# Holding each block of 128 queries in reverse, so that the relative-bias table loads from its 12 rows

## The chip, the cores and the metric

The kernel runs on one core of a Trainium2 chip. Times are device microseconds of one execution; lower is better. A core has TensorE (matmuls, PE in the profile; its weight loads are PEld), VectorE (DVE), ScalarE (ACT), GpSimd (POOL), and SyncE (SP), which here issues nearly all DMA transfers from one queue, in order.

## The reference

Two layers of an encoder over 256 tokens of 1024 channels, in float32. Each layer runs three token mixers side by side (differential attention with 4 heads, a gated DeltaNet, windowed attention with 8 heads), merges them, and then runs a gated MLP. The change concerns the bias that the two attentions add to their scores. It depends only on key position minus query position:

```python
rel = key_pos[None, :] - (start + jnp.arange(Q_BLOCK))[:, None]
bias = bias_table[t5_bucket(rel)].astype(jnp.float32).transpose(2, 0, 1)
p = jax.nn.softmax(s + bias[None, :, None], axis=-1)
```

There are 12 heads, so 12 rows of 511 different values. The windowed attention also masks distances over 128.

## The kernel before

**Work and precision.** All activations stay on the chip; the weights come from memory in blocks of 128 x 1024 floats (512 KB, the tile `raw`, three buffers). ScalarE rounds a block to `hi`, VectorE subtracts to get the residual `lo` (four buffers each), and TensorE multiplies each product in three passes (`mm3`). A block of a projection takes 24 matmuls of 256 columns. `weights` and `take` do this; their rows are `hi_take<-raw_take`, `lo_take<-raw_take,hi_take` and `mm_proj_ch`.

**Order.** Nothing is issued as it is written. `Plan` records every operation with a cost, dependencies and a rank, and `schedule` then lays out one order for all five engines; each engine runs its list in that order. `ORDER` gives the list of projections of each layer (the two lists are the same up to the eleventh entry and differ in a few places behind it), `PRIO` shifts ranks by label. A transfer from SP is priced by its output's elements, x 4 / 3.6e5 us, with 0.91 us until it lands; the blocks of weights are ahead of other transfers by `BOOST`. All lines of the profile are line 191, where the recorded call is made; so one goes by tiles.

**The bias table.** `bias_table` multiplies a one-hot matrix (33 x 512) by the table, copied eight times (`tbx`, 96 columns), so that the 12 rows lie on 96 partitions. Twelve transfers, one a head, then write each row 128 times into `skew` in device memory, with a pitch of 513 floats (256 KB a head). `load_G` reads it with a pitch of 512: each partition's row starts one element earlier than the one before, which is the shift from query to query. The result is a tile `G` of 128 queries x 384 keys (192 KB, two buffers), 24 times: 12 heads in each of two layers. Both blocks of queries read from the same tile, 128 columns apart.

**Where the queries go.** `stacked` copies the projected queries from PSUM into two tiles, q + residual stacked in the halves of the partitions. It serves the differential attention (tile `q_stacked`) and the window (`h_stacked`). In `attention` and `window` the scores of a block land with its queries on the partitions, VectorE adds G and takes the maximum, and after softmax and the product with the values the result is transposed back and written as a rounded half and a residual (`yh`, `yl`; tiles `ya_attention`, `yc_window`).

Of the kernel before, what the change touches and what calls it, by code (L numbers as in the profile page):

```python
# [10 lines left out]
F32 = mybir.dt.float32  # L11
# [4 lines left out]
ALU = mybir.AluOpType  # L16
# [3 lines left out]
P = 128  # L20
# [461 lines left out]
def tile_encoder_trunk(ctx: ExitStack, tc: tile.TileContext, a: dict, out: bass.AP, depth=DEPTH, tap=None):  # L482
    nc = tc.nc
    plan = Plan()
    A = plan.either(nc.scalar, nc.vector)
    tap_ = tap
    tap = lambda name, ap: tap_(name, ap, SY.dma_start) if tap_ else None
    V, S, G, TE, SY = [plan.engine(*e) for e in (("DVE", nc.vector), ("ACT", nc.scalar), ("POOL", nc.gpsimd), ("PE", nc.tensor), ("SP", nc.sync))]

    cp = ctx.enter_context(tc.tile_pool(name="cp", bufs=1))  # L490
# [4 lines left out]
    dp = ctx.enter_context(tc.tile_pool(name="dp", bufs=1, space=bass.MemoryType.DRAM))  # L495
# [4 lines left out]
    def nm(base):  # L500
        import sys
        f = sys._getframe(2)
        base = f"{base}_{f.f_code.co_name}{f.f_lineno}"
        counts[base] = counts.get(base, 0) + 1
        return f"{base}_{counts[base]}"
# [4 lines left out]
    def buf(tag, shape=(P, 512), dtype=F32):  # L510
        return plan.tile(mp, shape, dtype, tag, nm(tag), BUFS[tag])

    def small(cols, dtype=F32, tag=None):
        n = {"g16": 8, "bn": 2, "mv": 2, "ve": 2, "rs": 2, "nmr": 2, "g8": 1}.get(tag, 4)
        return plan.tile(sp, (P, cols), dtype, tag, nm("s"), n)
# [10 lines left out]
    def ps_at(shape=(P, 512), dtype=F32):  # L526
        return plan.tile(pm, shape, dtype, "at", nm("at"), BANKS["at"], True)
# [4 lines left out]
    def bc_mid(ap, n):  # L532
        return ap.unsqueeze(1).to_broadcast([ap.shape[0], n, ap.shape[1]])

    def bc_last(ap, n):
        return ap.unsqueeze(2).to_broadcast([ap.shape[0], ap.shape[1], n])

    def drow(ap, off, n):
        return bass.AP(ap.tensor, ap.offset + off, [[0, P], [1, n]])


    late = []

    def load(n, out, in_):

        late.append((SY.dma_start(out=out, in_=in_), LOADS[n - 9]))
# [18 lines left out]
    V.memset(nhalf, -0.5)  # L565


    skew = dp.tile([12, P * 513], F32, name="skew")

    def bias_table():  # L570
        oh = buf("yc", (33, 512))
        load(11, oh, a["onehot"])
        tb = cp.tile([33, 12], F32, name="tb")
        V.memset(tb[32:33, :], NEG)
        V.memset(tb[32:33, 0:4], 0.0)
        load(11, tb[0:32, :], a["rel_bias"])
        tbx = cp.tile([33, 8, 12], F32, name="tbx")
        V.tensor_copy(tbx, bc_mid(tb, 8))
        fps = ps_at()
        TE.matmul(fps[0:96, :], tbx.rearrange("p c h -> p (c h)"), oh, start=True, stop=True)  # L580
        fsb = buf("yc", (96, 512))
        A.copy(fsb, fps[0:96, :])
        for h in range(12):
            SY.dma_start(
                out=bass.AP(skew.tensor, skew.offset + h * P * 513, [[16 * 513, 8], [513, 16], [1, 512]]),
                in_=fsb[h:96:12, :].unsqueeze(1).to_broadcast([8, 16, 512]),
            )

    def load_G(h):
        t = buf("G", (P, 384))  # L590
        SY.dma_start(out=t, in_=bass.AP(skew.tensor, skew.offset + h * P * 513 + 127, [[512, P], [1, 384]]))
        return t


# [134 lines left out]
    def pow_nhalf(dst, src, n):  # L729
        G.tensor_tensor(dst, src, nhalf[:, 0:n], op=ALU.pow)  # L730
# [475 lines left out]
    HALVES = [slice(0, 64), slice(64, 128)]  # L1206

    def stacked(ps, tags):

        out = []  # L1210
        for g, tag in enumerate(tags):
            t = buf(tag, (P, 2, T), F32R)
            A.copy(t[HALVES[g]], ps[HALVES[g]])
            V.tensor_tensor(t[HALVES[1 - g]], ps[HALVES[g]], t[HALVES[g]].bitcast(F32), op=ALU.subtract)
            out.append(t)
        return out


    def attention(l, pr, ys):
        dq, dk, dl = [], [], []  # L1220
        for b in range(2):
            ps = yield "aq", b
            dq.append(stacked(ps, ("q", "q")))
            ps = yield "ak", b
            kh, kl = [[buf(PAIRS[b], (P, 2, T), F32R) for _ in range(2)] for _ in range(2)]
            for c, (t, u) in enumerate(zip(kh, kl)):
                for r in HALVES:
                    A.copy(t[r], ps[HALVES[c]])
                for r in HALVES:
                    V.tensor_tensor(u[r], ps[HALVES[c]], t[HALVES[c]].bitcast(F32), op=ALU.subtract)  # L1230
            dk.append(kh)
            dl.append(kl)
        dv = yield "av", 0
        yh = [buf("ya", (P, 2, T), F32R) for _ in range(2)]
        yl = [buf("ya", (P, 2, T), F32R) for _ in range(2)]
        for h in range(NH):
            plan.label = (l, "a", h)
            gt = load_G(h)
            es = []
            mx = small(4, tag="mx")  # L1240
            sm = small(4, tag="sm")
            for c in range(2):
                ps = ps_at((P, 2, T))
                e = buf("e", (P, 2, T))
                for s in range(2):
                    qb = 1 - s
                    q = dq[h // 2][c][:, h % 2, qb * P:(qb + 1) * P]
                    TE.matmul(ps[:, s], q, dk[h // 2][c][:, h % 2], start=True, stop=False)
                    TE.matmul(ps[:, s], q, dl[h // 2][c][:, h % 2], start=False, stop=True)
                for s in range(2):  # L1250
                    n = 2 * c + s
                    V.tensor_tensor_reduce(e[:, s], ps[:, s], gt[:, s * P:s * P + T], 1.0, NEG, ALU.add, ALU.max, mx[:, n:n + 1])
                V.tensor_scalar(mx[:, 2 * c:2 * c + 2], mx[:, 2 * c:2 * c + 2], -0.125, None, ALU.mult)
                for s in range(2):
                    n = 2 * c + s
                    S.activation(e[:, s], e[:, s], AF.Exp, scale=0.125, bias=mx[:, n:n + 1], accum_out=sm[:, n:n + 1])
                es.append(e)
            rs = small(4, tag="rs4")
            V.reciprocal(rs, sm)
            V.tensor_scalar(rs[:, 2:4], rs[:, 2:4], pr["nlam"], None, ALU.mult)  # L1260
            for s in range(2):
                A.scale(es[0][:, s], es[0][:, s], rs[:, s:s + 1])
                V.scalar_tensor_tensor(es[0][:, s], es[1][:, s], rs[:, 2 + s:3 + s], es[0][:, s], ALU.mult, ALU.add)
            pt = ps_at((P, 2, T))
            for s in range(2):
                for kb in range(2):
                    TE.transpose(pt[:, kb, (1 - s) * P:(2 - s) * P], es[0][:, s, kb * P:(kb + 1) * P], ident)
            aT = buf("aT", (P, 2, T))
            A.copy(aT, pt)
            po = ps_at((P, 2, P))  # L1270
            for qb in range(2):
                for kb in range(2):
                    TE.matmul(po[:, qb], aT[:, kb, qb * P:(qb + 1) * P], dv[kb][:, h * P:(h + 1) * P], start=kb == 0, stop=kb == 1)
            ss = small(2, tag="ss2")
            o = buf("o", (P, 2, P))
            for qb in range(2):
                S.activation(o[:, qb], po[:, qb], AF.Square, accum_out=ss[:, qb:qb + 1])
            V.tensor_scalar(ss, ss, 1.0 / P, RMS_EPS, ALU.mult, ALU.add)
            f = small(2, tag="f2")
            pow_nhalf(f, ss, 2)  # L1280
            V.tensor_tensor(o, po, bc_last(f, P), op=ALU.mult)
            py = ps_at((P, T))
            for qb in range(2):
                TE.transpose(py[:, qb * P:(qb + 1) * P], o[:, qb], ident)
            hs, ls = yh[h // 2][:, h % 2], yl[h // 2][:, h % 2]
            A.scale(hs, py, pr["subln"])
            V.scalar_tensor_tensor(ls, py, pr["subln"], hs.bitcast(F32), ALU.mult, ALU.subtract)
        tap(f"ya{l}", yh[0])
        tap(f"zza{l}", yl[0])
        ys[0] = yh, yl  # L1290


    def window(l, pr, ys):
        rows = HALVES
        sq = []
        for b in range(2):
            ps = yield "cq", b
# [4 lines left out]
        ps = yield "ckv", 0  # L1302
# [12 lines left out]
        yh = [buf("yc", (P, 2, T), F32R) for _ in range(2)]  # L1315
        yl = [buf("yc", (P, 2, T), F32R) for _ in range(2)]
        for t in range(4):
            plan.label = (l, "c", t)
            aTs = []
            for g in range(2):  # L1320
                h = g * 4 + t
                gt = load_G(NH + h)
                ps = ps_at((P, 2, T))
# [24 lines left out]
            po = ps_at((P, T))  # L1348
            for kb in range(2):
                for g in range(2):  # L1350
                    TE.matmul(po[g * 64:(g + 1) * 64], vt[:, kb, g * 64:(g + 1) * 64], aTs[g][:, kb], start=kb == 0, stop=kb == 1)
            hs, ls = yh[t // 2][:, t % 2], yl[t // 2][:, t % 2]
            A.copy(hs, po)
            V.tensor_tensor(ls, po, hs.bitcast(F32), op=ALU.subtract)
        tap(f"yc{l}", yh[0])
# [130 lines left out]
```

## Time and profile before

| | |
|---|---|
| three runs | 1022.42, 1021.48, 1022.13 us; median 1022.13 |
| profiled execution | 1024.28 us, its span 1022.6 us |
| mean granted TensorE clock in it | 0.994 |
| busy: TensorE, weight loads | 979.9 us, 912.4 us |
| busy: VectorE, ScalarE, GpSimd | 745.6, 577.7, 112.1 us |
| DMA | 168.55 MB, mean 165 GB/s, 4.19 MB of it written |

The span is what the profile covers of the execution; the rest lies around it. The profiled execution is one of its own, 2.15 us above the median. [...] Names in a row read out<-in, with the buffer numbers left out; x is the number of instructions.

### The profile page before, as it was taken

To read this page: it belongs to the slowest core of one execution; us is meant where nothing else is said; L and a number is where in the kernel's file an instruction comes from. 1 tells how busy PE (TensorE), PEld (TensorE's weight loads), DVE (VectorE), ACT (ScalarE), POOL (GpSimd) and SP (SyncE) were. 2 spreads that over 40 slices of the span, in tenths; PEclk is the share of its full clock that TensorE was granted. 3 is DMA by queue.
4 is the path that set the end of the run, shared out by engine and by line. 5 is a ranking of instruction groups with operands and counts; after the bars stand their busy time and mean duration, and the time that the engine had idled before them with its cause. 6 is when DMAs were issued, how large, how long until landed. Compare 5 with 4: busy or idle time off the path is not lost. (4 is left out here: it accounts for less than half of the span.)

```text
span 1022.6 us, 19176 instructions
## 1 busy us (share of the span) xinstructions
PE 979.9 (96%) x7598; PEld 912.4 (89%) x7598; DVE 745.6 (73%) x1327; ACT 577.7 (56%) x1024; POOL 112.1 (11%) x108
## 2 busy tenths in 40 slices
PE   7989999999998999999989999999999979999996
PEld 5889999998986999998869989999999869999885
DVE  6779977675489776665679998875657878666555
ACT  5647685676455565554435776766644626555432
POOL 0510002100005100000144200001000240000000
PEclk9999999999999999999999999999999999999998
DMA  7854433463563765565625444333546736566662
GB/s 227 254 184 128 141 108 130 138 201 123 170 226 121 217 204 185 184 186 185 207 82 165 145 132 140 94 114 123 181 136 195 232 138 193 181 186 184 188 198 67
DMA packets 51717, 168.55 MB, mean 165 GB/s; under 512 B 5835, under 2 KB 11355, under 8 KB 51628
## 3 DMA queue, kind: packets, MB, share of 16 engines
q1 hardware_dynamic: 50252, 162.91, 50.5%
q0 software_dynamic: 1376, 4.43, 1.5%
q8 instruction: 59, 0.97, 0.4%
q14 instruction: 30, 0.25, 0.1%
HBM read 163.12 MB, written 4.19 MB: 164 GB/s over the span
## 5 line engine op out<-in xcount | busy, mean ns | idle before, releaser
L191 PE MATMUL mm_proj_ch<-xTl,hi_take 128*128 128x256 f32 x1488 | 420.4, 286 | 4.5 <-DVE xTl L191 4.5
L191 PE MATMUL mm_proj_ch<-xTh,lo_take 128*128 128x256 f32 x1488 | 421.9, 286 | 1.1 <-DVE lo_take L191 1.1
L191 PE MATMUL mm_proj_ch<-xTh,hi_take 128*128 128x256 f32 x1488 | 421.8, 287 | 0.4 <-ACT hi_take L191 0.4
L191 DVE TENSOR_TENSOR lo_take<-raw_take,hi_take 128x1024 fp32r<-128x1024 f32 x219 | 271.9, 1247 | 124.4 <-ACT hi_take L191 113.9
L191 ACT ACTIVATE hi_take<-raw_take 128x1024 fp32r<-128x1024 f32 x213 | 225.6, 1059 | 240.7 <-PE mm_proj_ch L191 150.7
L191 PEld LDWEIGHTS mm_proj_ch<-xTl,hi_take 128*128 128x128 f32 x1488 | 283.8, 192 | 8.9 <-DVE xTl L191 5.8
L191 PEld LDWEIGHTS mm_proj_ch<-xTh,lo_take 128*128 128x128 f32 x1488 | 284.4, 192 | 3.9 <-DVE lo_take L191 2.5
L191 PEld LDWEIGHTS mm_proj_ch<-xTh,hi_take 128*128 128x128 f32 x1488 | 283.8, 192 | 2.1 <-ACT hi_take L191 0.8
L191 DVE TENSOR_TENSOR lo_proj_tok<-raw_proj_tok,hi_proj_tok 128x1024 fp32r<-128x1024 f32 x50 | 61.2, 1225 | 48.8 <-ACT hi_proj_tok L191 48.8
L191 ACT ACTIVATE hi_proj_tok<-raw_proj_tok 128x1024 fp32r<-128x1024 f32 x50 | 53.1, 1061 | 74.0 <-PE mm_run L191 33.8
L191 POOL TENSOR_TENSOR s_tail<-s_tail,nhalf 128x1 f32<-128x1 f32 x8 | 6.8, 854 | 370.8 <-DVE s_tail L191 370.8
L191 DVE SCALAR_TENSOR_TENSOR z_conv_silu<-mm_proj_ch,col_params,z_conv_silu 128x254 f32<-128x254 f32 (+1 forms) x96 | 39.8, 475 | 1.1 <-ACT z_conv_silu L191 1.0
L191 ACT ACTIVATE e_window<-e_window,s_window 128x256 f32<-128x256 f32 x57 | 27.2, 498 | 7.3 <-DVE s_window L191 7.2
L191 POOL DMA_DIRECT2D ya_ln_params<-in_lnp_dram x16 | 8.8, 552 | 188.8 <-PE mm_product L191 96.5
L191 DVE SCALAR_TENSOR_TENSOR g_product<-g_product,mm_product 128x512 f32<-128x512 f32 x24 | 16.3, 684 | 16.4 <-PE mm_product L191 16.2
L191 PE MATMUL mm_run<-hi_proj_tok,ile_encoder_trunk 128*128 128x512 f32 x88 | 27.3, 389 | 0.0
L191 PE MATMUL mm_run<-hi_proj_tok,tile_encoder_trunk 128*128 128x512 f32 x88 | 27.2, 389 | 0.0
L191 ACT ACTIVATE e_attention<-e_attention,s_attention 128x256 f32<-128x256 f32 x47 | 22.6, 500 | 4.8 <-DVE s_attention L191 4.8
L191 PE MATMUL mm_product<-yc_window,hi_take 128*128 128x256 f32 x128 | 24.1, 286 | 1.1 <-DVE yc_window L191 0.6
L191 PEld LDWEIGHTS <-h_solve 128*128 128x128 f16 x448 | 20.2, 97 | 5.6 <-issue 2.6
L191 PE MATMUL mm_product<-ya_attention,hi_take 128*128 128x256 f32 x128 | 24.4, 286 | 0.0
L191 PE MATMUL mm_product<-ya_gdn,hi_take 128*128 128x256 f32 x128 | 23.4, 283 | 0.0
(347 smaller groups left out, 1708.7 us busy)
## 6 DMA issues: line engine op xcount, KB each, us to landing
raw_take<-in_w_dram SPq DMA_DIRECT2D x226, 512.0 KB
raw_proj_tok<-in_w_dram SPq DMA_DIRECT2D x60, 512.0 KB
G_load_G<-skew SPq DMA_DIRECT2D x24, 192.0 KB
ya_ln_params<-in_lnp_dram POOLq DMA_DIRECT2D x16, 256.0 KB, 5.9
skew<-yc_bias_table SPq DMA_DIRECT2D x12, 256.0 KB
x<-in_xT_dram SPq DMA_DIRECT2D x4, 256.0 KB
x<-in_x_dram SPq DMA_DIRECT2D x2, 512.0 KB
out_dram<-x SPq DMA_DIRECT2D x8, 128.0 KB
```

The source lines that it names most:

```text
L191: op.ways.append((eng, lambda fn=fn, args=args, kw=kw: fn(*args, **kw), _cost(eng, name, outs, ins, args, kw), table))
```

## The change

The queries of each block of 128 are now kept in reverse order on the free axis. `flip` makes a view of a PSUM tile that runs backwards within each block, `blocks` a view of an SBUF tile cut into blocks; `stacked` copies through them, so partition p holds query 127 - p of its block. With that, partition p of `G` needs row elements p to p + 383, a step of +1 from partition to partition. That can be read straight from a row of 512 values: `skew` with its twelve spreads becomes `band`, 12 x 512, written by one transfer, and `load_G` reads with a step of one element in both dimensions. At the end of each head `yh` and `yl` are written through the same views, which puts the queries back in order. `tbx` is gone: the matmul uses the 12 columns of the table.

```diff
--- before.py
+++ after.py
@@ -538,6 +538,14 @@
     def drow(ap, off, n):
         return bass.AP(ap.tensor, ap.offset + off, [[0, P], [1, n]])
 
+    def blocks(ap):
+        return ap.rearrange("p a (b c) -> p a b c", c=P) if len(ap.shape) == 3 else ap.rearrange("p (b c) -> p b c", c=P)
+
+    def flip(ap):
+
+        step, n = ap.ap[-1]
+        return bass.AP(ap.tensor, ap.offset + (P - 1) * step, [list(d) for d in ap.ap[:-1]] + [[P * step, n // P], [-step, P]])
+
 
     late = []
 
@@ -565,7 +573,8 @@
     V.memset(nhalf, -0.5)
 
 
-    skew = dp.tile([12, P * 513], F32, name="skew")
+
+    band = dp.tile([12, 512], F32, name="band")
 
     def bias_table():
         oh = buf("yc", (33, 512))
@@ -574,21 +583,15 @@
         V.memset(tb[32:33, :], NEG)
         V.memset(tb[32:33, 0:4], 0.0)
         load(11, tb[0:32, :], a["rel_bias"])
-        tbx = cp.tile([33, 8, 12], F32, name="tbx")
-        V.tensor_copy(tbx, bc_mid(tb, 8))
         fps = ps_at()
-        TE.matmul(fps[0:96, :], tbx.rearrange("p c h -> p (c h)"), oh, start=True, stop=True)
-        fsb = buf("yc", (96, 512))
-        A.copy(fsb, fps[0:96, :])
-        for h in range(12):
-            SY.dma_start(
-                out=bass.AP(skew.tensor, skew.offset + h * P * 513, [[16 * 513, 8], [513, 16], [1, 512]]),
-                in_=fsb[h:96:12, :].unsqueeze(1).to_broadcast([8, 16, 512]),
-            )
+        TE.matmul(fps[0:12, :], tb, oh, start=True, stop=True)
+        fsb = buf("yc", (12, 512))
+        A.copy(fsb, fps[0:12, :])
+        SY.dma_start(out=band, in_=fsb)
 
     def load_G(h):
         t = buf("G", (P, 384))
-        SY.dma_start(out=t, in_=bass.AP(skew.tensor, skew.offset + h * P * 513 + 127, [[512, P], [1, 384]]))
+        SY.dma_start(out=t, in_=bass.AP(band.tensor, band.offset + h * 512, [[1, P], [1, 384]]))
         return t
 
 
@@ -1207,11 +1210,13 @@
 
     def stacked(ps, tags):
 
-        out = []
+
+        out, ps = [], flip(ps)
         for g, tag in enumerate(tags):
             t = buf(tag, (P, 2, T), F32R)
-            A.copy(t[HALVES[g]], ps[HALVES[g]])
-            V.tensor_tensor(t[HALVES[1 - g]], ps[HALVES[g]], t[HALVES[g]].bitcast(F32), op=ALU.subtract)
+            h = [blocks(t[r]) for r in HALVES]
+            A.copy(h[g], ps[HALVES[g]])
+            V.tensor_tensor(h[1 - g], ps[HALVES[g]], h[g].bitcast(F32), op=ALU.subtract)
             out.append(t)
         return out
 
@@ -1282,7 +1287,7 @@
             py = ps_at((P, T))
             for qb in range(2):
                 TE.transpose(py[:, qb * P:(qb + 1) * P], o[:, qb], ident)
-            hs, ls = yh[h // 2][:, h % 2], yl[h // 2][:, h % 2]
+            hs, ls, py = blocks(yh[h // 2][:, h % 2]), blocks(yl[h // 2][:, h % 2]), flip(py)
             A.scale(hs, py, pr["subln"])
             V.scalar_tensor_tensor(ls, py, pr["subln"], hs.bitcast(F32), ALU.mult, ALU.subtract)
         tap(f"ya{l}", yh[0])
@@ -1349,7 +1354,7 @@
             for kb in range(2):
                 for g in range(2):
                     TE.matmul(po[g * 64:(g + 1) * 64], vt[:, kb, g * 64:(g + 1) * 64], aTs[g][:, kb], start=kb == 0, stop=kb == 1)
-            hs, ls = yh[t // 2][:, t % 2], yl[t // 2][:, t % 2]
+            hs, ls, po = blocks(yh[t // 2][:, t % 2]), blocks(yl[t // 2][:, t % 2]), flip(po)
             A.copy(hs, po)
             V.tensor_tensor(ls, po, hs.bitcast(F32), op=ALU.subtract)
         tap(f"yc{l}", yh[0])
```

## Rows read from the trace of the kernel before

**Rows 1.** Part 1 of the page: engine, busy us, share, instructions.
```profile
PE 979.9 (96%) x7598; PEld 912.4 (89%) x7598; DVE 745.6 (73%) x1327; ACT 577.7 (56%) x1024; POOL 112.1 (11%) x108
```

**Rows 2.** Windows: length, busy us (instructions) by engine, TensorE clock, DMA share, GB/s.
```profile
52.00:55.00 3.00, 3.00 (x27) 3.00 (x26) 2.36 (x2) 1.54 (x2) 0.00 (x0) 1.00 0.65 197
55.00:58.00 3.00, 2.47 (x21) 2.27 (x19) 0.00 (x0) 0.13 (x1) 0.00 (x0) 1.00 0.94 315
58.00:61.00 3.00, 0.05 (x1) 0.05 (x1) 1.98 (x3) 2.35 (x4) 0.00 (x0) 1.00 0.56 204
61.00:64.00 3.00, 3.00 (x14) 3.00 (x15) 2.97 (x7) 1.06 (x1) 0.00 (x0) 0.50 0.65 216
...
75.00:100.00 25.00, 24.13 (x278) 22.95 (x277) 23.79 (x47) 18.19 (x28) 2.79 (x3) 1.00 0.35 111
```

**Rows 3.** Timeline, TensorE, 52 to 66 us: start, us, idle before and its releaser.
```profile
57.19 0.28 PE L191 MATMUL mm_proj_ch<-xTh,hi_take 128*128 128x256 f32 x1
60.95 1.23 PE L191 MATMUL at_attention<-s_attention,q_stacked 128*128 128x256 f32 x4 [3.48 <-DVE q_stacked L191]
```

**Rows 4.** Timeline, VectorE, 22 to 72 us.
```profile
58.96 1.23 DVE L191 TENSOR_TENSOR lo_take<-raw_take,hi_take 128x1024 fp32r<-128x1024 f32 x1 [4.18 <-ACT hi_take L191]
60.21 1.41 DVE L191 TENSOR_TENSOR q_stacked<-mm_proj_ch,q_stacked 64x512 fp32r<-64x512 f32 x2
```

**Rows 5.** Timeline, ScalarE, 22 to 72 us.
```profile
57.87 1.06 ACT L191 ACTIVATE hi_take<-raw_take 128x1024 fp32r<-128x1024 f32 x1 [4.10 <-DMA raw_take<-in_w_dram]
58.95 0.59 ACT L191 ACTIVATE q_stacked<-mm_proj_ch 64x512 fp32r<-64x512 f32 x1
```

**Rows 6.** Timeline, SP's queue, 22 to 72 us and from 1008 us.
```profile
45.45 2.38 SPq L191 DMA_DIRECT2D skew<-yc_bias_table  x3
49.21 0.33 SPq L191 DMA_DIRECT2D raw_take<-in_w_dram  x1
49.59 1.39 SPq L191 DMA_DIRECT2D skew<-yc_bias_table  x2
...
1009.18 10.95 SPq L191 DMA_DIRECT2D out_dram<-x  x8
```

**Rows 7.** DMA, 27 to 62 us: total, then issues with KB each.
```profile
DMA packets 3358, 8.80 MB, mean 251 GB/s; under 512 B 286, under 2 KB 542, under 8 KB 3356
...
raw_take<-in_w_dram SPq DMA_DIRECT2D x9, 512.0 KB
skew<-yc_bias_table SPq DMA_DIRECT2D x12, 256.0 KB
```

**Rows 8.** Waits, TensorE, 540 to 660 us, longest: us, times, longest one.
```profile
PE ch_solve L191 <- ACT h_solve L191: 1.2, 4, 0.4
```

**Rows 9.** Tile tbx: duration ns min/median/max, first and last start.
```profile
L191 DVE COPY tbx<-tb x1: 192/192/192, 26.1 to 26.1; 33x96 f32<-33x96 f32 x1
```

**Rows 10.** Windows around one bias load, then during the parameters' load.
```profile
621.00:621.50 0.50, 0.50 (x7) 0.50 (x6) 0.47 (x2) 0.00 (x0) 0.00 (x0) 1.00 0.85 80
621.50:622.00 0.50, 0.50 (x6) 0.50 (x6) 0.47 (x2) 0.00 (x0) 0.00 (x0) 1.00 0.85 316
...
294.00:294.50 0.50, 0.50 (x4) 0.41 (x3) 0.50 (x2) 0.50 (x2) 0.00 (x0) 1.00 0.90 188
```

**Rows 11.** Tile G_load_G: idle time of its readers, us, times.
```profile
  DMA G_load_G<-skew: 0.8, 1
```

**Rows 12.** Groups by form, ScalarE and VectorE: count, busy us, mean ns.
```profile
L191 ACT ACTIVATE h_solve<-ch_solve 32x256 f16<-32x256 f32 x16 | 6.0, 373 | 0.3
...
L191 ACT ACTIVATE q_stacked<-mm_proj_ch 64x512 fp32r<-64x512 f32 x8 | 4.7, 588 | 0.1
...
L191 ACT ACTIVATE s_window<-mm_proj_ch 64x256 fp32r<-64x256 f32 x8 | 3.0, 374 | 0.1
...
L191 DVE TENSOR_TENSOR q_stacked<-mm_proj_ch,q_stacked 64x512 fp32r<-64x512 f32 x8 | 5.5, 688 | 0.2
```

## Prediction

> **What bounds the kernel now.** I read the page first: TensorE is busy 979.9 us of a 1022.6 us span [rows 1], so some 43 us at most can be won by removing waits. The table is built and spread early in the first layer, so I cut the stretch around and behind that into slices of 3 us [rows 2]. TensorE runs 27 matmuls in a slice when it is fed (52 to 55). [...] Measured in matmuls the hole is (27-21) + (27-1) + (27-14) = 45, at 3/27 = 0.111 us each 5.0 us: about 3.5 us of standing still and 1.5 us of half clock.
>
> Which wait ends last there? The timeline of TensorE shows its last matmul before the hole at 57.19 and the next at 60.95, after 3.48 us of waiting for VectorE's subtraction that writes the stacked queries [rows 3]. On VectorE that subtraction starts at 60.21, queued behind the residual of a weight block at 58.96 [rows 4]; ScalarE's half of the stacked queries, at 58.95, is queued behind the rounding of the same block, which began at 57.87 after 4.10 us of waiting for its DMA [rows 5]. So the root is one weight block that came late: SP issued it at 49.21, and it was used 8.66 us later. Just ahead of it in SP's queue are three spreads (from 45.45), and two more follow at 49.59 [rows 6]. Between 27 and 62 us the engines moved 8.80 MB; in it are nine weight blocks (4.72 MB) and the twelve spreads (3.15 MB) [rows 7]. In the slices around the late block the DMA share is 0.94, 0.56 and 0.65 [rows 2]: the block stands in a full queue, and the spreads are 36% of what is in it.
>
> **The change part by part.** *Twelve spreads go, one 24 KB store comes.* Without the spreads 5.7 MB are left in the same 35 us, 161 GB/s, where the engines reach 315 in one of these very slices [rows 2]. Nothing is then left to make the block of 49.21 late, and the chain of [rows 3 to 6] is gone. In layer 1, whose list of projections is nearly the same and where no spread runs, TensorE's largest wait between 540 and 660 us is a solver step, 1.2 us in four pieces of at most 0.4; the stacked queries stop nothing [rows 8]. I take the 5.0 us as won, less 0.3 us for what copy and subtraction may still need between the last matmul and the first score: -4.7. Bounds: -5.0 with nothing remaining, -3.5 with a queue of one residual (1.2 us) and the rest of a subtraction. SP's issue time for the spreads, 2.38 us for three [rows 6], is saved too, but SP stands waiting for free buffers anyway: nothing.
>
> [...] The trace shows 0.94 of the engines busy in the slice where the block is late [rows 2]. [...] No row here shows single engines.
>
> *The table itself.* The copy tbx goes, 0.19 us of VectorE [rows 9]. The matmul has 12 columns held instead of 96, with the same 512 moving, and the eviction the same 512 columns: nothing. The 0.19 us lie beside a busy TensorE; without that cover they would be worth 0.2 us.
>
> *A new wait.* The first bias load now stands right behind the one store, and SP waits until that store has landed. The nearest row is the end of the kernel: SP's last issue of an output store ends at 1020.13 and the span at 1022.6 [rows 6], so 2.5 us at most. Queued behind it on SP is the next weight block, and ScalarE waits for that. A block is issued three buffers ahead of its use, and TensorE needs 24 x 0.111 = 2.7 us for each, so some 8 us cover 2.5 us and the landing. Cost 0; bounds 0 and 2.5 us, the second only if TensorE has no other block in hand. [...]
>
> *Bias loads from one row.* There are 24 loads of 192 KB. Before, 128 partitions read 128 different rows; after, all read one 2 KB row, each 4 bytes further on. A load of before moves its 197 kB within 1.0 us (80 and 316 GB/s in two half microseconds); the nearest row for many readers of one row are the normalisation parameters, 188 GB/s at a share of 0.90, beside other traffic [rows 10]. 197 kB at 188 GB/s are 1.05 us, at 316 they are 0.62: so 0 to +0.43 us a load. It costs only where a load is used as soon as it lands; before, VectorE waited for one once, 0.8 us [rows 11]. I take +0.3 us in all; bounds 0 and rival 3.
>
> *Reversed PSUM reads.* ScalarE and VectorE each read 16 half tiles of 512 columns and 16 tiles of 256 columns backwards, in runs of 128. Forwards, a half tile takes 588 ns on ScalarE and 688 ns on VectorE; no row of before reads backwards. Runs with gaps cost nothing: 256 columns in runs of 32 take 373 ns, 256 in one run 374 ns [rows 12]. The upper bound is half rate: some 0.45 us more for each half tile and 0.22 us for each of the others, 11 us on each engine; from 75 to 100 us VectorE is busy 23.79 of 25 [rows 2], so a part of it, some 3 us, would come through. I take 0, since a direction is nearer to a gap than to a halved rate.
>
> *The order.* The program plans the order of all instructions itself, and prices a spread at 65,536 x 4 / 3.6e5 = 0.73 us of SP. Twelve of these leave its plan, so the order behind 29 us can come out otherwise, in the first layer above all, and open or close waits. Bounds: the 1.2 us of the solver's waits [rows 8] closing in one layer or both, against a second hole of 5.0 us. I take 0.
>
> Sum: -4.7 + 0.3 = -4.4 us. The profiled execution took 1024.28 us (1.68 us outside its span) and would take 1019.9; the median of the runs shown is 2.15 us below it, so 1022.13 - 4.4 = **1017.7 us**.
>
> **The rivals.** (1) *The hole shrinks but stays.* The rounding of a block also needs a buffer that TensorE frees, so ScalarE and VectorE could hold the stacked queries back without any DMA. For it: the queries are queued behind that block's work on both engines [rows 4, 5]. Against: layer 1 [rows 8]. With 3 of the 5.0 us left it gives 1022.1 - 2.0 = 1020.1. (2) *The new order opens another hole.* For it: VectorE is the full engine from 75 to 100 us [rows 2], and one residual out of turn stops TensorE. Against: only SP's part of the plan changes directly. One hole of the same 5.0 us cancels the gain: 1022.1 - 4.4 + 5.0 = 1022.7, 2 us either way. (3) *Bias loads come late*: slower than before. The place is the window heads of both layers, 16 loads that follow one another with little lead. At +0.43 us a load, the second of a pair waiting for the first as well, a pair costs 0.43 + 0.86 = 1.3 us and eight pairs 10.3 us: 1022.1 - 4.7 + 10.3 = 1027.7. The gain is used up from 4.7 / 24 = 0.2 us a load on. For it: a load was waited for once already [rows 11]. Against: the others were not, and the row of the parameters had other traffic beside it. (4) *Backward reads run at half rate*: 1022.1 - 4.4 + 3 = 1020.7, and up to 1024 where the queries are stacked ahead of the first scores as well.
>
> **How the numbers follow.** Forecast 0.56, rival 1 0.10, rival 2 0.17, rival 3 0.09, rival 4 0.08. About 0.2%, 2 us, is what a measurement of this kernel can tell from no change. Faster: the forecast, half of rival 1 and 0.02 of rival 2 = 0.63. Slower: rival 3, a third of rival 4 and 0.08 of rival 2 = 0.20. The same: 0.17. The likeliest case alone spans 1016.2 (the whole 5.0 us, and the 0.87 us that TensorE stands between 75 and 100 us [rows 2], since VectorE comes there earlier) to 1019.5 (the -3.5 of the hole with late loads beside it). The range goes down to 1014.5 for solver waits that close in both layers and up to 1025 for rivals 1, 2 and 4; most of rival 3 lies above it, and with it a part of rival 2 and of the low side, some 2 in 10.
>
> **What would show it.** Right: no slice between 50 and 70 us below a granted clock of 1.00, no wait of TensorE for the stacked queries above 1 us, 3.1 MB fewer written, ScalarE's waits for weight DMAs in that stretch near zero; the first bias load within 3 us of the store; the reversed copies at 588 and 688 ns. Wrong: a hole of 3 us is back elsewhere in the first 300 us, or VectorE waits for bias tiles more than twice, or those copies are longer.

## The result and the profile after

The changed kernel takes 1016.96 us (median of six, 1013.42 to 1018.16) beside 1022.27 us for the kernel before in the same runs: ratio 0.995, 95% interval 0.9938 to 0.9963, 5.3 us by the medians. Run again on another chip it gave 0.9969 (0.9954 to 0.9984), 3.2 us. The forecast was 1017.7 us, 4.4 us less. The profiled execution took 1016.10 us with a span of 1014.4 us.

First the same slices of TensorE as [rows 2], and those where something new stands. View: windows of the kernel after (columns as in [rows 2]).

```profile
55.00:58.00 3.00, 3.00 (x27) 3.00 (x27) 2.10 (x4) 2.99 (x6) 0.00 (x0) 1.00 0.36 135
58.00:61.00 3.00, 3.00 (x28) 3.00 (x27) 3.00 (x8) 2.22 (x3) 0.00 (x0) 1.00 0.60 180
61.00:64.00 3.00, 3.00 (x28) 3.00 (x27) 3.00 (x4) 2.27 (x7) 0.00 (x0) 1.00 0.47 143
...
76.00:79.00 3.00, 1.03 (x7) 0.63 (x6) 3.00 (x9) 2.97 (x5) 0.00 (x0) 1.00 0.00 0
79.00:82.00 3.00, 2.96 (x23) 2.66 (x24) 2.95 (x5) 1.99 (x4) 0.00 (x0) 0.60 0.54 173
82.00:85.00 3.00, 3.00 (x43) 2.83 (x43) 2.93 (x5) 1.71 (x3) 0.00 (x0) 0.83 0.55 176
```

The hole at 55 to 64 us is gone: 27 to 28 matmuls in every slice at a granted clock of 1.00, where [rows 2] has 21, 1 and 14, the last at 0.50. Another stands at 76 to 82 us: 7 matmuls, then 23 at a granted clock of 0.60. The DMA engines move nothing in the first of these slices, so this one has no transfer behind it. The timelines say what it has. TensorE:

```profile
77.14 0.39 PE L191 MATMUL mm_proj_ch<-xTh,hi_take 128*128 128x256 f32 x1 [0.72 <-ACT hi_take L191]
...
78.88 0.39 PE L191 MATMUL mm_proj_ch<-xTh,lo_take 128*128 128x256 f32 x1 [1.24 <-DVE lo_take L191]
```

VectorE, same kernel and stretch:

```profile
73.85 1.17 DVE L191 COPY h_solve<-id 128x1024 f16<-128x1024 f16 x2
74.94 0.68 DVE L191 TENSOR_TENSOR nl_solve<-N_decay,h_solve 128x512 f16<-128x512 f32 x1
75.54 2.15 DVE L191 SCALAR_TENSOR_TENSOR N_decay<-ch_gdn,nbeta_gdn_scalars,N_decay 128x128 f32<-128x128 f32 x8
77.61 1.21 DVE L191 TENSOR_TENSOR lo_take<-raw_take,hi_take 128x1024 fp32r<-128x1024 f32 x1
```

VectorE works without a gap from 73.85 us on, and the residual of a weight block stands behind 4 us of solver preparation. TensorE waits 0.72 us for ScalarE's rounding and 1.24 us for this residual, 1.97 us in the slice (3.00 less 1.03). The lower clock of the next two slices takes at most another 0.40 x 3 + 0.17 x 3 = 1.7 us, by my estimate from the two granted clocks: 2.0 to 3.7 us in all. The second trace of this kernel has the same two waits (0.72 and 1.23 us), at a granted clock of 1.00 up to 85 us. The planner's order differs from that of the kernel before in about the first quarter of VectorE's and ScalarE's lists; the lists of layer 1 are the same.

What else the prediction named, each from its own view of the kernel after. DMA, 27 to 62 us (beside [rows 7]):

```profile
DMA packets 1836, 5.97 MB, mean 171 GB/s; under 512 B 219, under 2 KB 475, under 8 KB 1833
...
raw_take<-in_w_dram SPq DMA_DIRECT2D x10, 512.0 KB, 3.6
```

Waits of ScalarE, 26 to 62 us (9.9 us in four waits before, the longest of them the 4.10 us of [rows 5]):

```profile
ACT hi_take L191 <- DMA raw_take<-in_w_dram: 0.9, 1, 0.9
```

SP's queue, 22 to 36 us, and under it SP's waits:

```profile
22.91 2.70 SPq L191 DMA_DIRECT2D raw_take<-in_w_dram  x3
25.65 0.39 SPq L191 DMA_DIRECT2D band<-yc_bias_table  x1
30.26 0.80 SPq L191 DMA_DIRECT2D G_load_G<-band  x2
```

```profile
SPq L191 <- DMA band<-yc_bias_table: 4.2, 1, 4.2
```

Groups by form (beside [rows 12]) and the waits for the bias tiles (beside [rows 11]):

```profile
L191 DVE TENSOR_TENSOR q_stacked<-mm_proj_ch,q_stacked 64x512 fp32r<-64x512 f32 x8 | 5.5, 690 | 0.2
...
L191 ACT ACTIVATE q_stacked<-mm_proj_ch 64x512 fp32r<-64x512 f32 x8 | 4.7, 587 | 0.1
```

```profile
  DMA G_load_G<-band: 1.7, 3
...
DMA to landing us min/median/max: 3.0/3.5/5.1
```

2.83 MB less move in that stretch, over the whole kernel 1.07 MB are written instead of 4.19, the weight blocks come in time, and backward reads take 587 and 690 ns where forward ones took 588 and 688. Three signs went the other way: SP waited 4.2 us for the store, so that the first bias load starts 4.6 us behind it; VectorE waited three times for a bias tile, where more than twice was named as a sign of being wrong; and the hole at 76 us comes near the 3 us that were named as another.

### The profile page after: what moved, and what is told of

It reads as the page before. It is cut to its first block, busy times and chain, and to the rows that moved or that the text cites. A ratio compares the mean times of both kernels' runs of the same rounds, so it can differ in the third digit from the quotient of the medians.

```text
span 1014.4 us, 19166 instructions
## 1 busy us (share of the span) xinstructions
PE 977.3 (96%) x7598; PEld 909.8 (90%) x7598; DVE 744.0 (73%) x1324; ACT 578.1 (57%) x1026; POOL 113.6 (11%) x108
## 3 DMA queue, kind: packets, MB, share of 16 engines
HBM read 163.12 MB, written 1.07 MB: 162 GB/s over the span
## 5 line engine op out<-in xcount | busy, mean ns | idle before, releaser
L191 PEld LDWEIGHTS mm_proj_ch<-xTh,lo_take 128*128 128x128 f32 x1488 | 279.7, 189 | 5.5 <-DVE lo_take L191 4.1
L191 PEld LDWEIGHTS mm_proj_ch<-xTl,hi_take 128*128 128x128 f32 x1488 | 279.2, 189 | 5.7 <-DVE xTl L191 3.4
L191 PEld LDWEIGHTS mm_proj_ch<-xTh,hi_take 128*128 128x128 f32 x1488 | 279.7, 189 | 2.6 <-ACT hi_take L191 1.6
L191 POOL TENSOR_TENSOR x<-q_tail,ya_ln_params 128x512 f32<-128x512 f32 x12 | 22.2, 1865 | 11.2 <-DVE q_tail L191 11.2
```

Of the source, the lines that this page charges most:

```text
L191: op.ways.append((eng, lambda fn=fn, args=args, kw=kw: fn(*args, **kw), _cost(eng, name, outs, ins, args, kw), table))
```

## Experiments

All ratios are to the kernel before on the same chip. To hold the order fixed, some kernels let the planner see the operations of one kernel and put another transfer in their place:

```python
def instead(i, call):
    op = plan.ops[i]
    op.ways = [(op.ways[0][0], call, op.ways[0][2], op.ways[0][3])]
```

In "old order" kernels TensorE, VectorE, ScalarE and GpSimd have the very lists of the kernel before; in "new order" kernels those of the changed one.

**Old order, no spreads.** The change without its re-planning.

```diff
+            def call(h=h):
+                if h == 0:
+                    nc.sync.dma_start(out=band, in_=fsb[0:12, :])
+            instead(i, call)
...
+        instead(i, lambda: nc.sync.dma_start(out=t, in_=bass.AP(band.tensor, band.offset + h * 512, [[1, P], [1, 384]])))
```

> The kernel computes as the changed one does (reversed queries, bias tiles read from the 12 rows), but every engine keeps the order of the kernel before: the planner still prices the twelve spreads, and at their places nothing is issued (the first place holds the one store). Theory 1, the queue: the hole of 5.0 us between 55 and 64 us goes because the weight blocks land in time, and the time is about 1017.5 us, as for the changed kernel. Rival, the order: the gain came from the new order, so with the old order the hole stays and the time is within 2 us of 1022. Third reading, which the trace of the changed kernel suggests (TensorE stands still for 2 us at 76 us and its granted clock is 0.60 to 0.83 until 85 us): the new order gave some 2.5 to 3 us back, so the old order without spreads is faster than the changed kernel, about 1014.5 us.

Measured: 1017.15 us, ratio 0.9975 (0.9963 to 0.9987). The hole is gone, and none stands at 76 us, but the 1014.5 us of the third reading did not come. Windows of this run:

```profile
55.00:58.00 3.00, 3.00 (x27) 3.00 (x26) 2.57 (x4) 1.43 (x4) 0.00 (x0) 1.00 0.88 280
58.00:61.00 3.00, 3.00 (x27) 3.00 (x26) 3.00 (x9) 1.31 (x2) 0.00 (x0) 1.00 0.52 202
61.00:64.00 3.00, 3.00 (x28) 3.00 (x27) 3.00 (x5) 1.49 (x3) 0.00 (x0) 1.00 0.28 83
76.00:79.00 3.00, 3.00 (x27) 3.00 (x26) 3.00 (x9) 1.71 (x3) 0.00 (x0) 1.00 0.50 175
```

**Old order with spreads.** The same, and the twelve spreads run where they ran before, into memory that nobody reads.

```diff
                 if h == 0:
                     nc.sync.dma_start(out=band, in_=fsb[0:12, :])
+                spread()
```

> As the run before it, in the old order, but the twelve spreads are issued where the kernel before issues them, with the same source and shape, into memory that nobody reads; the bias tiles still come from the 12 rows and the queries are still reversed. Theory 1: all of the gain hangs on the traffic, so the hole of about 5 us between 55 and 64 us is back and the time is within 2 us of 1022. If reversed reads or loads from one row cost or give anything by themselves, it shows here as the difference to the kernel before: 0 by the prediction, 3 us or more by its rivals on them. Rival, the order: no hang on the traffic, the same time as the run without spreads.

Measured: 1022.44 us, ratio 1.0024 (1.0012 to 1.0035). Windows, then from the timelines TensorE's wait in the hole and ScalarE's rounding ahead of it:

```profile
55.00:58.00 3.00, 1.40 (x12) 1.19 (x10) 0.80 (x1) 1.84 (x3) 0.00 (x0) 1.00 0.91 311
58.00:61.00 3.00, 1.80 (x11) 1.79 (x12) 2.90 (x6) 1.42 (x3) 0.00 (x0) 0.86 0.72 211
61.00:64.00 3.00, 3.00 (x18) 3.00 (x17) 3.00 (x7) 0.35 (x2) 0.00 (x0) 0.57 0.24 90
```

```profile
59.20 0.74 PE L191 MATMUL at_attention<-s_attention,q_stacked 128*128 128x256 f32 x4 [2.80 <-DVE q_stacked L191]
...
56.12 1.06 ACT L191 ACTIVATE hi_take<-raw_take 128x1024 fp32r<-128x1024 f32 x1 [3.42 <-PE mm_proj_ch L191]
```

12 + 11 + 18 in place of 81 matmuls: 40 x 0.111 = 4.4 us, back with the spreads and nothing else. TensorE waits for the stacked queries again. This trace puts ScalarE's wait down to TensorE, not to the DMA; but without the spreads the same rounding starts after TensorE's 283rd matmul and here after its 313th, so no buffer of TensorE held it. Nor was it SP's time for issuing the spreads: SP stood idle for 1.8 us, waiting for a buffer, right before it issued this block at 48.13 us. By the medians of the two runs on one chip the spreads cost 5.3 us, by the ratios 0.49%, 5.0 us. That is the relief; but the run is 0.24% above the kernel before, so something in the rest of the change takes 2.4 us, at this order.

**Reversal alone, row loads alone.** Which part takes it? The first keeps the twelve spreads and their rows (pitch 511) and reverses the queries:

```diff
+                out=bass.AP(skew.tensor, skew.offset + h * P * 513, [[16 * 511, 8], [511, 16], [1, 511]]),
+                in_=fsb[h:96:12, 0:511].unsqueeze(1).to_broadcast([8, 16, 511]),
...
+        out, ps = [], flip(ps)
```

> The kernel before with one part of the change: the queries held in reverse (the backward reads of stacked, attention and window). The twelve spreads stay where they were; their pitch is 511 instead of 513, so that a load still reads 128 different rows, now with a step of +1 from query to query. The lists of TensorE, VectorE, ScalarE and GpSimd are those of the kernel before. Theory A (direction is free, as the copies' durations of 588 and 688 ns say): 1022.3, ratio 1.000 within 0.0015, with the hole at 55 to 64 us. Theory B (the +2.4 us of old order with spreads comes from the backward reads): ratio 1.0024, about 2.4 us more, and then some of the 32 reversing instructions on each engine are longer by 0.08 us or more.

The second is old order with spreads, without `flip` and `blocks`.

> The other part alone: the 24 bias loads read from the 12 rows (128 readers of one 2 KB row, one more store of 24 KB), the twelve spreads stay and go to memory that nobody reads, and the queries are not reversed, so that the bias added is not the reference's. The lists of the four engines are those of the kernel before. Theory A (the +2.4 us of old order with spreads is the one-row loads and the store): ratio 1.002 to 1.0025, and VectorE waits for bias tiles 2 times or more, with 1 us in all. Theory B (the loads are free, the backward reads cost): ratio 1.000. If this and the reversal alone are both at 1.000 to 1.001, the +2.4 us were scatter between chips.

Measured: reversal 1.0001 (0.9982 to 1.002); row loads 1.0024 (1.0007 to 1.004). Backward reads cost nothing that shows: the interval leaves 2 us either way, and the copies keep their durations. The 2.4 us come with the loads from one row and their store. In the trace they can't be pointed at: VectorE's waits for bias tiles in the run with row loads are

```profile
  DMA G_load_G<-band: 1.0, 2
```

and none with the reversal alone, and the one wait of TensorE for VectorE between 640 and 735 us is 0.4 us.

**The changed kernel again.**

> The changed kernel once more, on the chip of the other runs of this set, as a control for the old order without spreads (0.9975 of the kernel before). If the new order is worth something by itself: 0.995. If the difference between the two was scatter between chips: 0.9965 to 0.998.

Measured: 0.9969 (0.9954 to 0.9984). It lies within the interval of the old order without spreads, so the new order is worth between nothing and the 2.5 us by which the first measurement (0.995) was better. In layer 0 it is no better at all: the first matmul of `mm_run`, which stands behind the mixers of that layer, starts at 289.1 us (289.3 in the first trace) and at 287.8 us with the old order without spreads.

**New order with spreads**, two behind each of six weight blocks, from 8 adjacent partitions.

```diff
+            in_=x.rearrange("p a b -> p (a b)")[0:8, 0:512].unsqueeze(1).to_broadcast([8, 16, 512]),
```

> The order of the changed kernel, and beside it twelve spreads of the same shape into memory that nobody reads, two behind each of six weight blocks after the store. Theory 1, the queue: the blocks of 30 to 55 us come 4 to 5 us late again; the new order has the stacked queries' copies at other places, so the hole need not be at the same place, but 3 us or more are lost: 1020 us or more. Rival, the order: the time stays within 2 us of 1017.

Measured: 1.0368 (1.0348 to 1.0387), far outside what the spreads' bytes could explain. Windows of this run:

```profile
43.00:46.00 3.00, 1.10 (x10) 0.89 (x8) 0.00 (x0) 0.53 (x1) 0.91 (x2) 1.00 0.47 124
46.00:49.00 3.00, 0.58 (x4) 0.58 (x5) 1.92 (x2) 2.80 (x5) 0.00 (x0) 1.00 0.65 96
49.00:52.00 3.00, 1.95 (x11) 1.65 (x9) 0.00 (x0) 0.00 (x0) 0.00 (x0) 0.54 0.56 93
```

The queue moves 93 to 124 GB/s where the kernel before, with spreads of the same size in its queue, moved 228 to 300 GB/s in these three slices.

**New order, spreads from partitions 12 apart**, as the kernel before has them.

```diff
-            in_=x.rearrange("p a b -> p (a b)")[0:8, 0:512]...
+            in_=x.rearrange("p a b -> p (a b)")[h:96:12, 0:512]...
```

> The changed kernel's order with twelve spreads of 256 KB put back, two behind each of six weight blocks, into memory that nobody reads; their source is 8 partitions that lie 12 apart, as in the kernel before (the run with the new order and spreads had 8 adjacent partitions). Theory A (traffic alone makes the hole, wherever the order puts it): 0.5% above the changed kernel, so 0.999 to 1.001 of the kernel before, with a hole of 4 to 5 us of TensorE between 40 and 75 us. Theory B (the new order would have carried the spreads): 0.995 to 0.996. Theory C (the 3.7% of the run with adjacent partitions came from the place of the spreads in the queue and not from the source): again over 1.03. If A or B holds, adjacent source partitions made that run slow.

Measured: 1.0012 (0.9995 to 1.0028), against 0.9969 for the changed kernel on the same chip: 0.43%, 4.4 us. So the spreads cost nearly the same in either order, and what made the run ahead of this one slow was the source. Two things differ there: the distance of the partitions, and that all twelve spreads of that run took the same 8 partitions, where here each has its own. (The two kernels with 16 partitions below use one set each for all twelve, so between them only the distance differs.) Windows, two of the worst slices ahead of the new order's own hole, which now stands at 82 us:

```profile
49.00:52.00 3.00, 1.55 (x14) 1.35 (x12) 0.00 (x0) 0.98 (x1) 0.00 (x0) 1.00 0.72 264
...
67.00:70.00 3.00, 2.03 (x10) 2.03 (x11) 2.78 (x3) 2.98 (x12) 0.00 (x0) 0.70 0.43 158
```

**Sixteen in the slowest dimension.** A spread of before goes from 8 partitions, 16 copies each. Does that division make the block late? Two kernels give the same bytes a slowest dimension of 16, with the old order; the first from 16 adjacent partitions, the second from 16 that lie 6 apart.

```diff
+                out=bass.AP(skew.tensor, skew.offset + h * P * 513, [[8 * 513, 16], [513, 8], [1, 512]]),
+                in_=fsb[0:16, :].unsqueeze(1).to_broadcast([16, 8, 512]),
...
-                in_=fsb[0:16, :].unsqueeze(1)...
+                in_=fsb[0:96:6, :].unsqueeze(1)...
```

> As the second run, but each spread takes its rows from 16 partitions, 8 copies each, instead of 8 partitions and 16 copies: the same bytes, rows and places. If the number of bytes makes the blocks late, nothing changes against the second run (within 2 us of 1022, the hole between 55 and 64 us as deep). [...]

> The order of the kernel before with loads from the 12 rows and twelve spreads of the same 256 KB into memory that nobody reads, each now from 16 partitions that lie 6 apart, 8 copies each (before: 8 partitions that lie 12 apart, 16 copies each). [...] Theory B (bytes in the queue make the hole, however they are divided): 1.0015 to 1.003 and the hole of 4 to 5 us. If it is over 1.005, as with 16 adjacent partitions (1.008), the place of the source was not what made that run slow.

Measured: adjacent 1.008 (1.0064 to 1.0096), apart 1.0023 (1.0009 to 1.0037). The second equals the run with 8 (1.0024), and its hole is no smaller: 35 matmuls in the three slices, 41 there. Windows of the second:

```profile
55.00:58.00 3.00, 1.25 (x11) 1.05 (x9) 0.78 (x1) 1.82 (x3) 0.00 (x0) 1.00 0.88 194
58.00:61.00 3.00, 1.78 (x8) 1.79 (x9) 2.90 (x6) 1.73 (x3) 0.00 (x0) 0.56 0.84 258
61.00:64.00 3.00, 3.00 (x16) 3.00 (x15) 3.00 (x7) 0.00 (x0) 0.00 (x0) 0.50 0.20 79
```

So 8 in place of 16 is not what makes the block late; no run shows single engines. Adjacent partitions cost again: 1.008 beside 1.0023.

**Row starts that move.** Loads from one row also start 4 bytes further on in each partition. This kernel is the one with the reversal alone, spreads with a pitch of 512 and loads with one of 513: own rows, moving starts.

> As the run with the reversal alone, but the spreads have a pitch of 512 and the loads one of 513: each partition still reads a row of its own, and its start moves on by 4 bytes from partition to partition, as in the changed kernel. The lists of the four engines are those of the kernel before; the bias is the reference's. Theory A (the +2.4 us of the loads from one row, 1.0024 twice, is 128 readers of the same 2 KB): 1.000, as with the reversal alone (1.0001), and no wait of VectorE for bias tiles above 0.8 us in all. Theory B (it is the starts that move by 4 bytes): 1.002 to 1.0025, with 2 or more waits for bias tiles.

Measured: 0.9974 (0.9964 to 0.9985), which neither theory gave. No wait for a bias tile is left in the trace; whether the moving starts cost time can't be read off the ratio, since the spreads' rows moved in the same run. With these rows 2,048 bytes apart the hole shrank. Windows, and DMA from 27 to 62 us, with all twelve spreads in it:

```profile
55.00:58.00 3.00, 3.00 (x26) 2.85 (x24) 0.89 (x2) 1.61 (x2) 0.00 (x0) 1.00 0.88 322
58.00:61.00 3.00, 1.60 (x13) 1.54 (x13) 2.91 (x6) 1.94 (x4) 0.00 (x0) 1.00 0.82 308
61.00:64.00 3.00, 3.00 (x27) 3.00 (x27) 3.00 (x8) 1.31 (x2) 0.00 (x0) 1.00 0.21 83
```

```profile
DMA packets 3514, 9.36 MB, mean 268 GB/s; under 512 B 307, under 2 KB 563, under 8 KB 3511
```

15 matmuls are missing, 1.7 us, and the clock doesn't fall. ScalarE waits 3.0 us for weight blocks there; with the pitch of 511 it was 7.1 us at 253 GB/s, and with 513 it was 9.9 us at 251 [rows 7] (4.1 and 8.1 us, at 251 and 250 GB/s, in the two other traces with that pitch and the same source).

**Fewer readers of a row.** The changed kernel, its order kept, with each row stored eight times and 16 partitions reading each copy.

```diff
+            out=band.rearrange("h (c n) -> h c n", c=8),
+            in_=fsb.unsqueeze(1).to_broadcast([12, 8, 512]),
...
+            out=t, in_=bass.AP(band.tensor, band.offset + h * 8 * 512, [[528, 8], [1, 16], [1, 384]])))
```

> The changed kernel with its order unchanged, but the one store writes each of the 12 rows eight times (192 KB instead of 24 KB), and each load reads its 128 partitions from these eight rows, 16 from each. Theory A (128 readers of one row cost 2.4 us): 2 us below the changed kernel (0.9969 and 0.995 of before), so 0.993 to 0.995, with landings of a bias load below the 3.7 us median and fewer waits for them (2.4 us, 4 times). Theory B (the number of readers of a row is no matter): 0.995 to 0.997, landings and waits as they were. The larger store should land within 1 us of the small one.

Measured: 0.9966 (0.9953 to 0.9978), no gain. The tile view of `G_load_G` in this run shows a price of the form itself: SP needs 602 ns to issue such a load, where the other form takes 327.

```profile
L603 SPq DMA_DIRECT2D G_load_G<-band x24: 574/602/607, 31.4 to 722.5; - x24
...
  DMA G_load_G<-band: 3.4, 4
```

**Own rows, no spreads.** The changed kernel, its order kept; each load reads 128 rows of a weight block, so what is added is not the bias, and no load waits for the store.

```diff
+        instead(i, lambda: nc.sync.dma_start(out=t, in_=a["w"][h][:, 0:384]))
```

> The changed kernel with its order unchanged; only the source of the 24 bias loads differs: the first 384 columns of a weight block, so that each of the 128 partitions reads a row of its own, 4 KB from the next. What is added to the scores is then not the bias. Theory A (loads from one row cost the changed kernel about 2.4 us, as they did beside the spreads): 0.9925 to 0.9945, VectorE's waits for bias tiles at 0.8 us or below. Theory B (without the spreads the one-row loads cost nothing that reaches TensorE): 0.995 to 0.997 as the changed kernel, whatever becomes of VectorE's waits (1.7 and 2.4 us).

Measured: 0.9947 (0.9934 to 0.9961), between the two theories. Tile view:

```profile
  DMA G_load_G<-in_w_dram: 0.3, 1
...
DMA to landing us min/median/max: 2.8/3.3/5.3
```

A load lands 0.2 to 0.4 us sooner than from one row (medians of 3.5 and 3.7 us in the two traces of the changed kernel), and VectorE's waits fall from 1.7 and 2.4 us to 0.3. The interval overlaps both measurements of the changed kernel, so what this is worth in time stays open between 0 and 2.2 us. The stage of layer 1 in which ten of the 24 loads are issued shows nothing: from the first `mm_token_major` matmul of layer 1 to the first `mm_run` are 281.4 us here, 280.6 and 280.8 us in the changed kernel's traces.

## Why the prediction was right, point by point

The time came out at 1016.96 for 1017.7 us, with the sign and the cause as forecast. The smaller terms had other sizes than given, and that the sum came so close is in part luck.

*The hole* (-4.7, bounds -5.0 and -3.5): right. With all four lists fixed, the spreads in or out change the time by 0.49%, 5.0 us, and in the new order by 0.43%, 4.4 us. The chain was the one named: with the spreads gone ScalarE's wait for weight blocks goes from 9.9 to 0.9 us and the 3.48 us for the stacked queries [rows 3] are not among TensorE's waits. Rival 1 (hole stays without a DMA) is out: with the old order and no spreads there are 27 and 28 matmuls in each slice.

*The table itself* (0): right. Its matmul took 593 ns with 12 columns held and 628 with 96 (medians of two, the shortest 589 in both), its eviction 587 and 577 ns.

*The reversed reads* (0): right. 587 and 690 ns, ratio 1.0001 (0.9982 to 1.002); rival 4 is out. Its half rate was my assumption, which no run showed.

*The loads from one row* (+0.3): mis-sized beside the spreads. The price of one load was within its bounds (0 to +0.43 us; measured 0.2 to 0.4 us in landing), but three kernels with these loads and spreads lay at 1.0024, 1.0024 and 1.0023, 2.4 us. Rival 3 is out at its price: three waits for bias tiles, 1.7 us, no 10 us. Whether the 2.4 us are the readers of one row or the store that goes ahead isn't settled: the odd pitch left no wait for a bias tile, which speaks against moving starts without excluding them, eight rows in place of one bought nothing, and own rows without spreads gave 0 to 2.2 us. No single wait of TensorE holds them.

*The new wait of SP* (0, bound 2.5 us): the bound was too low. SP stands for 4.2 us (4.5 us in the second trace). I had read it off the end of the kernel, where a store has the queue nearly to itself (66 GB/s from 1015 to 1023 us); here three blocks of 512 KB were issued just ahead. The DMA engines are 0.91 busy from 28 to 29 us and stand idle from 30 us, when the wait ends; but no run takes these blocks away, so that they are the reason is argued. The cover held: between 30 and 46 us TensorE's listed waits are 1.1 us for `x_decay` and none for a block, 0.8 us before.

*The order* (0): the step that I had least ground for. Rival 2's mechanism did happen, with VectorE as the full engine and a residual out of turn, as it was described: 2 us of waiting at 76 us, and up to 3.7 us with the clock. It didn't decide: the whole of the new order against the old one came out between 0 and -2.5 us, and the trace of layer 0 shows no gain by it (289.1 and 289.3 against 287.8 us). At the old order the change is thus worth -2.5 us (0.9975): -5.0 for the traffic and, taken from another kernel and chip (row loads alone, 1.0024), +2.4 for the loads. The full change has 0.995 and 0.9969; the 0.6 to 2.5 us between are the order or scatter between chips, and that stays open. The forecast's -4.4 has the right main term, and its two mis-sized small ones, the loads and the order, partly cancel: that is the luck in it.

## What to carry to other kernels

When a transfer is removed, look at who stood behind it in its queue and price that stall, not the bytes, with the lower clock behind it where the trace shows one: 0.50 in the kernel before, 0.86 and 0.57 in the old order with spreads, but 1.00 with the rows 2,048 bytes apart. Measure a change of a planned kernel with the old order held fixed too: here the data path alone gave 0.9975, and a new hole of 2 us or more came from the order alone. Where such writes must stay, take their source from partitions that lie apart (1.0012 for 1.0368 with 8, 1.0023 for 1.008 with 16), and try rows 2,048 bytes apart: in one run, in which the pitch of the loads changed too, this went with a gain of 2.7 us, about half of what the spreads cost.

## What the runs showed of the hardware

With twelve stores of 256 KB from the same 8 adjacent partitions the queue moved 93 to 124 GB/s in the slices shown and a mean of 101 GB/s from 46 to 88 us, and the kernel took 1.0368; from 8 that lie 12 apart the time was 1.0012. With 16 adjacent partitions it was 1.008, with 16 that lie 6 apart 1.0023. The mean busy share of the DMA engines was 0.55 in the run with 8 adjacent ones (46 to 88 us) and 0.92 with 16 (46 to 70 us). Why adjacent partitions cost is not shown; no run shows single engines.

With the same stores in rows 2,048 bytes apart, all transfers of 27 to 62 us made a mean of 268 GB/s, in rows 2,044 or 2,052 bytes apart 253 and 251 GB/s; the time went from 1.0001 (pitch of 2,044 bytes) to 0.9974, with one kernel each and on two chips. The pitch of the loads changed with that of the stores, so which of the two did it is not shown; the loads, from starts that moved on by 4 bytes a partition in the run with 268 GB/s, left no wait for a bias tile.
